# A third x buffer: all three state projections ahead of the tables and the latent tiles

## The chip, the cores and the metric

One core of a Trainium2 chip runs the kernel. The metric is device time in microseconds (us) of one execution, the median of several runs. The core has five engines with a queue each, which run their own instructions in order and wait for each other by semaphores: PE (matrix products), DVE (VectorE), ACT (ScalarE), POOL (GpSimd), and SP (SyncE), which here only issues DMA transfers. PEld is PE's loading of weights.

## What is computed

One step of a streaming encoder layer over 1152 positions (1024 of a new stream, 8 running streams with 16 each), all in float32:

```
xn  = RMSNorm(x)                         # x: 1152 x 1024
hin = xn @ w_in                          # -> q latent 384 | kv latent 256 | rope key 32 | S5 channels u 512
c_q, c_kv = RMSNorm(q_lat), RMSNorm(kv_lat)
o_a = attention(c_q, c_kv, rope key)     # 8 heads, chunk mask; running streams with their cache
bu  = B_bar u                            # S5: 32 groups of 16 channels, 64 complex states each
s   = associative_scan(lambda_bar, bu)   # over positions
o_b = GLU(gelu(Re(C s) + D u))
h   = x + concat(o_a, o_b) @ w_out
y   = h + ConvFFN(RMSNorm(h))
```

The change touches the first phase: the input projection `xn @ w_in`, the S5 tables (lambda_bar, B_bar and products of them) and the start of the S5 scan.

## The kernel before

A matmul operand is held as two halves, `hi` (rounded) and `lo` (the rest), and each product is three matmuls: hi hi, lo hi, hi lo (`mm3`, L138). `split` (L102, then L105 or L123) writes hi on ACT and lo on DVE or POOL.

Positions are cut into three blocks of 384 (block 2 holds the new stream's last 256 positions and the 128 of the running streams) and into nine latent tiles of 128 (block b has tiles 3b to 3b+2). `phase_a` works on transposed x:

- `load_x(b, k)` loads slice k of 8 of block b (`xs`, three buffers), splits it into `xhi`, `xlo` and sums squares into `accx`; `stats(b)` makes the norm factors `rx` and the row `Rb`.
- `load_w(k, hi, lo, c0)` loads slice k of the weights (`ws`, two buffers) and splits it. `wuh`, `wul` hold the 512 state columns, `wnh`, `wnl` the 672 latent columns. lo goes to DVE for even k and to POOL for odd k.
- `upart(b)` is the state projection of a block: 96 matmuls into four `up` banks, times `Rb` into `us` (two buffers) on DVE, stored to `u_dram`.
- `natpart(i)` is latent tile i: 48 matmuls into two `nat` banks, evicted by ACT, squares and square roots on ACT, two rsqrt chains of five small DVE steps each, two scalings on DVE, the rotation of `kpe` on POOL, stores to `cq_dram`, `ckv_dram` and the output. `nat` has two buffers.
- `tables()` makes the S5 tables: a long chain of small DVE steps, then products on POOL and DVE (`epre`, `tmpE`; `fo`, `tmpF`), PE transposes and products (`ep`, `kp`), stores to `e_dram`, `f_dram`, `kt_dram`.
- `s5_early` opens the tiles `Et` and `U` in the memory that the tables leave and loads `Et` from `e_dram`; `s5_load_u` loads `U` from `u_dram` in eight transfers (one for each position of a chunk of eight).
- `s5_states` makes the products `pst` of Et and U and evicts them into `RI` (`RI` on ACT and DVE, L423). Then `s5_scan` runs on DVE and POOL (steps `w`, `RI` at L105). `b8_open` and `b8_q` prepare the running streams' queries.

In the program the order is: load x 2 with wu, load x 0, load wn, `upart(2)`, `upart(0)`, tables, `s5_early`, latent tiles 8, 7, 6, load x 1 into the buffer that block 2 leaves, `upart(1)`, `s5_load_u`, `s5_states`, latent tiles 0 to 5 with b8 after tile 2. Blocks 2 and 1 share one buffer, block 0 has its own.

A scheduler that runs when the kernel is built moves instructions of one engine against each other, as their inputs come in its own model of time, and so the queues differ from the program text: the first steps of the tables, say, run among the x splits. Within a queue the order is then fixed. A tile that opens in memory that another has left waits for the last reader of that.

Of the kernel before, what the change touches and what calls it, by code (L numbers as in the profile page):

```python
# [75 lines left out]
def build(tc, t):  # L76
# [4 lines left out]
    with root:  # L81
# [43 lines left out]
        def split(hi, lo, src, scale=None, eng=None):  # L125
            if scale is None:
                acopy(hi, src)
                sub(lo, src, hi, eng)
            else:
                acopy(hi, src, scale)  # L130
                stt(lo, src, scale, hi.bitcast(F32), ALU.mult, ALU.subtract)
# [488 lines left out]
        def phase_a():  # L620
            st = ExitStack()
            with st:
                a = st.enter_context(tc.tile_pool(name="a", bufs=1))
                sg = st.enter_context(tc.tile_pool(name="asg", bufs=2))
                xb = None
                wnh = a.tile([P, 8, NATW], F32R, name="wnh")
                wnl = a.tile([P, 8, NATW], F32R, name="wnl")
                xhl, accx, al = {}, {}, {}

                def load_x(b, k):  # L630
                    if k == 0:
                        xp = xb if b == 0 else a
                        xhl[b] = (xp.tile([P, 8, TB], F32R, tag="xhi", name="xhi"),
                                  xp.tile([P, 8, TB], F32R, tag="xlo", name="xlo"))
                    s = al["p"].tile([P, TB], F32, tag="xs", name="xs", bufs=XB[0])
                    load(s, t["xT"][k * P:(k + 1) * P, b * TB:(b + 1) * TB])
                    split(xhl[b][0][:, k], xhl[b][1][:, k], s, gmix[:, k:k + 1])
                    if k == 0:
                        accx[b] = al["p"].tile([P, TB], F32, tag="accx", name="accx", bufs=1)
                        nc.scalar.activation(out=accx[b], in_=s, func=AF.Square)  # L640
                    else:
                        q = al["p"].tile([P, TB], F32, tag="sqx", name="sqx")
                        nc.scalar.activation(out=q, in_=s, func=AF.Square)
                        add(accx[b], accx[b], q, nc.gpsimd if b == 0 else None)

                def load_w(k, hi, lo, c0):
                    n = hi.shape[2]
                    w = al["p"].tile([P, NATW], F32, tag="ws", name="ws", bufs=XB[1])
                    load(w[:, 0:n], t["w_in"][k * P:(k + 1) * P, c0:c0 + n])
                    split(hi[:, k], lo[:, k], w[:, 0:n], eng=nc.gpsimd if k % 2 else None)  # L650

                gkv = a.tile([P, KL], F32, name="gkv")
                ss = a.tile([P, NT], F32, name="ss")
# [19 lines left out]
                def upart(b, kouter=False):  # L673
# [4 lines left out]
                    def step(cb_, k):  # L678
                        c0 = cb_ * P
                        if k == 0:  # L680
                            pu[cb_] = psum("u", [P, TB], "up")
                        mm3(pu[cb_], [((wuh[:, k, c0:c0 + P], wul[:, k, c0:c0 + P]), (xh[:, k], xl[:, k]))], first=k == 0, last=k == 7)

                    if kouter:
                        for k in range(8):
# [12 lines left out]
                def natpart(i):  # L698
# [6 lines left out]
                    jk = sg.tile([P, QL], BF16, tag="jk2", name="jk2", bufs=1)  # L705
                    for z, (c0, c1) in enumerate(((0, QL), (QL, NATW))):
                        p_ = psum("s", [P, c1 - c0], "nat")
                        mm3(p_, [((xh[:, k, tsl], xl[:, k, tsl]), (wnh[:, k, c0:c1], wnl[:, k, c0:c1])) for k in range(8)])
                        acopy(n[:, c0:c1], p_, rx[:, i:i + 1])
                        w = (QL, KL)[z]  # L710
                        nc.scalar.activation(out=jk[:, 0:w], in_=n[:, c0:c0 + w], func=AF.Square, accum_out=sq[:, z:z + 1])
                        rsqrt_act(sg, rq[:, z:z + 1], sq[:, z:z + 1], 1.0 / w, f"rq{z}")
                    cq, ck = n[:, 0:QL], n[:, QL:QL + KL]
                    ts(cq, cq, rq[:, 0:1], None, ALU.mult)
                    store(cq_dram[i * P:(i + 1) * P], cq)
# [10 lines left out]

                xbs = ExitStack()
                al["p"] = xbs.enter_context(tc.tile_pool(name="asl", bufs=2, reuse_waits="tile"))
                xb = xbs.enter_context(tc.tile_pool(name="xb", bufs=1, reuse_waits="tile"))
                ust = ExitStack()  # L730
                au = ust.enter_context(tc.tile_pool(name="au", bufs=1))
                wuh = au.tile([P, 8, SW], F32R, name="wuh")
                wul = au.tile([P, 8, SW], F32R, name="wul")
                for k in range(8):
                    load_x(2, k)
                    load_w(k, wuh, wul, NATW)
                load(ident, t["ident"])
                stats(2)
                for k in range(8):
                    load_x(0, k)  # L740
                late_consts()
                load(gkv, t["g_kv"])
                stats(0)
                for k in range(8):
                    load_w(k, wnh, wnl, 0)
                upart(2, True)
                upart(0, True)
                tables()
                s5_early()
                for i in (8, 7, 6):  # L750
                    natpart(i)
                for k in range(8):
                    load_x(1, k)
                stats(1)
                upart(1)
                ust.close()
                s5_open()
                s5_load_u()
                s5_states()
                for i in range(6):  # L760
                    natpart(i)
# [962 lines left out]
```

## Time and profile before

| | us |
|---|---|
| runs | 1563.75, 1566.25, 1566.29; median 1566.25 |
| the profiled execution | 1564.88 |
| its span, first to last instruction | 1563.1 |
| PE busy | 1470.5 (94%) |
| DVE busy | 1114.7 (71%) |
| ACT busy | 680.1 (44%) |
| POOL busy | 328.3 (21%) |
| mean granted clock of PE | 0.972 |

The span is cut into stages by time: up to some 58 us the x and weight splits with the first state projections, to 118 us the tables, to 175 us the third state projection and the first products of the S5 states, to 265 us the scan, and behind that attention, output projection and the ConvFFN, which is the larger part of the span. Busy times of an engine count instructions that run, also while such an instruction waits for a port; an idle engine that bounds nothing costs nothing. The granted clock is 1.00 at 2.4 GHz and 0.50 at 1.2 GHz.

### The profile page before, as it was taken

To read this page: it belongs to the slowest core of one execution; us is meant where nothing else is said; L and a number is where in the kernel's file an instruction comes from. 1 tells how busy PE (TensorE), PEld (TensorE's weight loads), DVE (VectorE), ACT (ScalarE), POOL (GpSimd) and SP (SyncE) were. 2 spreads that over 40 slices of the span, in tenths; PEclk is the share of its full clock that TensorE was granted. 3 is DMA by queue.
4 is the path that set the end of the run, shared out by engine and by line. 5 is a ranking of instruction groups with operands and counts; after the bars stand their busy time and mean duration, and the time that the engine had idled before them with its cause. 6 is when DMAs were issued, how large, how long until landed. Compare 5 with 4: busy or idle time off the path is not lost.

```text
span 1563.1 us, 23843 instructions
## 1 busy us (share of the span) xinstructions
PE 1470.5 (94%) x8733; PEld 1416.5 (91%) x8733; DVE 1114.7 (71%) x2372; ACT 680.1 (44%) x1323; POOL 328.3 (21%) x624
## 2 busy tenths in 40 slices
PE   6896866999989999999999999999999999999998
PEld 6876755877878999999999999999999999999998
DVE  8984799475778876468676666777767777667766
ACT  6342346666667886335333333333333333333321
POOL 3560466230355322112100000000000000000000
PEclk9998867999999999999999999999999999999999
DMA  7449434463221322630021111111111111111103
GB/s 201 123 150 153 126 122 87 100 199 103 79 91 49 95 72 77 212 101 28 25 71 41 42 41 41 42 51 44 43 50 44 41 41 41 42 41 41 41 1 132
DMA packets 101460, 122.15 MB, mean 78 GB/s; under 512 B 39524, under 2 KB 81636, under 8 KB 100868
## 3 DMA queue, kind: packets, MB, share of 16 engines
q1 hardware_dynamic: 100960, 120.44, 27.2%
q8 instruction: 68, 1.11, 0.3%
q14 instruction: 48, 0.39, 0.1%
q0 software_dynamic: 384, 0.20, 0.1%
HBM read 93.95 MB, written 26.65 MB: 77 GB/s over the span
## 4 chain that ended last, share of the span: by engine, by line
PE 76%; DVE 13%; DMA 5%; ACT 2%; issue 2%; SPq 2%; POOL 0%; DVEq 0%; ACTq 0%; POOLq 0%
PE pu L138 36%; PE pd L138 17%; PE pw L138 6%; DVE w L105 3%; PE pk L138 2%; PE pg L138 1%; PE pq L138 1%; PE po L1255 1%; SPq L96 1%; PE pst L1242 1%; PE pst L1243 1%; PE pst L1244 1%; PE po L1254 1%; PE po L1253 1%; DMA U<-u_dram 1%
## 5 line engine op out<-in xcount | busy, mean ns | idle before, releaser
L105 DVE TENSOR_TENSOR hT<-hT,pd 128x384 f32<-128x384 f32 x528 | 288.3, 551 | 218.4 <-PE pd L138 218.2
L138 PE MATMUL pu<-hnh,wh 128*128 128x384 f32 x1056 | 356.6, 338 | 0.0
L138 PE MATMUL pu<-hnl,wh 128*128 128x384 f32 x1056 | 356.4, 338 | 0.0
L138 PE MATMUL pu<-hnh,wl 128*128 128x384 f32 x1056 | 356.1, 337 | 0.0
L138 PE MATMUL pd<-act,wh 128*128 128x384 f32 x1056 | 348.7, 336 | 0.5 <-DVE hT L105 0.4
L1525 ACT ACTIVATE c<-pu,cvh 128x384 f32<-128x384 f32 x132 | 88.7, 672 | 309.0 <-PE pu L138 308.8
L138 PEld LDWEIGHTS pd<-act,wh 128*128 128x128 f32 x1056 | 197.7, 188 | 2.4 <-DVE hT L105 2.3
L138 PEld LDWEIGHTS pu<-hnh,wh 128*128 128x128 f32 x1056 | 198.4, 188 | 0.0
L138 PEld LDWEIGHTS pu<-hnl,wh 128*128 128x128 f32 x1056 | 198.3, 188 | 0.0
L138 PEld LDWEIGHTS pu<-hnh,wl 128*128 128x128 f32 x1056 | 198.0, 188 | 0.0
L123 DVE SCALAR_TENSOR_TENSOR c<-u,cvh,c 128x256 f32<-128x256 f32 (+1 forms) x352 | 171.2, 517 | 26.9 <-ACT u L102 13.7
L138 PE MATMUL pd<-act,wl 128*128 128x384 f32 x528 | 177.4, 336 | 0.0
L102 ACT ACTIVATE act<-c 128x384 fp32r<-128x384 f32 x66 | 34.7, 525 | 158.5 <-DVE c L105 158.5
L1531 POOL COPY u<-u 128x2 f32<-128x2 f32 x88 | 19.9, 227 | 384.6 <-DVE c L105 174.0
L138 PEld LDWEIGHTS pd<-act,wl 128*128 128x128 f32 x528 | 99.2, 188 | 0.0
L105 DVE TENSOR_TENSOR wl<-ws,wh 128x1024 fp32r<-128x1024 f32 x74 | 92.0, 1248 | 7.9 <-ACT wh L102 7.9
L102 ACT ACTIVATE wh<-ws 128x1024 fp32r<-128x1024 f32 x74 | 77.9, 1056 | 15.2 <-PE pw L138 8.8
L1543 POOL COPY cvo<-u 128x2 f32<-128x2 f32 x44 | 8.1, 184 | 355.2 <-ACT u L102 355.2
L1547 ACT ACTIVATE c<-c 128x384 f32<-128x384 f32 x66 | 34.6, 525 | 74.8 <-DVE c L123 74.7
L102 ACT ACTIVATE u<-pu 128x384 f32<-128x384 f32 (+2 forms) x176 | 66.3, 405 | 0.0
L138 PE MATMUL pw<-oh,wh 128*128 128x384 f32 x192 | 65.0, 340 | 0.2 <-DVE ql L123 0.2
L138 PE MATMUL pw<-oh,wl 128*128 128x384 f32 x192 | 64.4, 336 | 0.0
(461 smaller groups left out, 3122.9 us busy)
## 6 DMA issues: line engine op xcount, KB each, us to landing
ws<-in_w_up SPq DMA_DIRECT2D x44, 512.0 KB, 3.6
ws<-in_w_down SPq DMA_DIRECT2D x22, 512.0 KB, 3.5
xs<-in_xT SPq DMA_DIRECT2D x24, 192.0 KB, 3.5
os<-o_dram SPq DMA_DIRECT2D x24, 192.0 KB, 2.7
hT<-in_xT SPq DMA_DIRECT2D x24, 192.0 KB, 4.5
out_yT<-hT SPq DMA_DIRECT2D x24, 192.0 KB, 2.1
cf<-in_cT SPq DMA_DIRECT2D x8, 512.0 KB, 4.0
cn<-in_cn SPq DMA_DIRECT2D x8, 512.0 KB, 5.6
```

The costliest lines, as they stand in the source:

```text
L96: nc.sync.dma_start(out=out, in_=in_)
L102: nc.scalar.activation(out=out, in_=in_, func=AF.Copy, scale=scale)
L105: (eng or nc.vector).tensor_tensor(out=out, in0=a, in1=b, op=op)
L123: nc.vector.scalar_tensor_tensor(out=out, in0=a, scalar=s, in1=b, op0=op0, op1=op1)
L138: nc.tensor.matmul(out, lhsT=w, rhs=x, start=first and i == 0, stop=last and i == n - 1)
L1242: nc.tensor.matmul(o_, lhsT=kh[0:r, 4 * g + h, ks], rhs=qh[0:r, h, qs_], start=True, stop=False)
L1243: nc.tensor.matmul(o_, lhsT=kl[:, 4 * g + h, ks], rhs=qh[0:QD, h, qs_], start=False, stop=False)
L1244: nc.tensor.matmul(o_, lhsT=kh[0:QD, 4 * g + h, ks], rhs=ql[:, h, qs_], start=False, stop=True)
L1253: nc.tensor.matmul(po[:, qs_], lhsT=vhs, rhs=ph[:, sc_], start=f, stop=False)
L1525: nc.scalar.activation(out=c, in_=p_, func=AF.Identity, scale=w[2], bias=w[3])
L1531: nc.gpsimd.tensor_copy(out=u[:, 0:2], in_=halo[i, gv][:, TB:TB + 2])
L1547: nc.scalar.activation(out=g_, in_=g_, func=AF.Silu)
```

## The change

There is a third buffer for x, so that no block waits for another. The two halves of the weights are now lists of eight tiles each, one for a slice k and half; the state and the latent weights have the same tags (`wh0` and so on), so that slice k of the latent weights takes the memory of slice k of the state weights when its last projection has read that. In the program all x loads and all three state projections now come first, then the latent weights, the tables, `s5_early`, `s5_load_u`, and then the latent tiles 8, 7, 6; `s5_open`, `s5_states` and the tiles 0 to 5 follow as before. In `natpart` the two rsqrt chains are one chain over both columns; the square of a column is scaled before it is summed.

```diff
+                xpool = {1: a}
+                def wtiles(n, nm):
+                    return [[a.tile([P, n], F32R, tag=f"w{y}{k}", name=f"{nm}{y}{k}", padded_shape=[P, NATW]) for k in range(8)] for y in "hl"]
...
-                        xp = xb if b == 0 else a
+                        xp = xpool[b]
...
-                        nc.scalar.activation(out=jk[:, 0:w], in_=n[:, c0:c0 + w], func=AF.Square, accum_out=sq[:, z:z + 1])
-                        rsqrt_act(sg, rq[:, z:z + 1], sq[:, z:z + 1], 1.0 / w, f"rq{z}")
+                        nc.scalar.activation(out=jk[:, 0:w], in_=n[:, c0:c0 + w], func=AF.Square, scale=w ** -0.5, accum_out=sq[:, z:z + 1])
+                    rsqrt_act(sg, rq, sq, 1.0, "rq")
...
-                ust = ExitStack()
-                au = ust.enter_context(tc.tile_pool(name="au", bufs=1))
-                wuh = au.tile([P, 8, SW], F32R, name="wuh")
-                wul = au.tile([P, 8, SW], F32R, name="wul")
+                x2s = ExitStack()
+                xpool[2] = x2s.enter_context(tc.tile_pool(name="xc", bufs=1, reuse_waits="tile"))
+                wu = wtiles(SW, "wu")
                 for k in range(8):
                     load_x(2, k)
-                    load_w(k, wuh, wul, NATW)
+                    load_w(k, wu[0], wu[1], NATW)
                 load(ident, t["ident"])
                 stats(2)
                 for k in range(8):
                     load_x(0, k)
+                stats(0)
+                upart(2, True)
                 late_consts()
                 load(gkv, t["g_kv"])
-                stats(0)
-                for k in range(8):
-                    load_w(k, wnh, wnl, 0)
-                upart(2, True)
-                upart(0, True)
-                tables()
-                s5_early()
-                for i in (8, 7, 6):
-                    natpart(i)
                 for k in range(8):
                     load_x(1, k)
                 stats(1)
-                upart(1)
-                ust.close()
+                upart(0, True)
+                upart(1, True)
+                wn = wtiles(NATW, "wn")
+                for k in range(8):
+                    load_w(k, wn[0], wn[1], 0)
+                tables()
+                s5_early()
+                s5_load_u()
+                for i in (8, 7, 6):
+                    natpart(i)
+                x2s.close()
                 s5_open()
-                s5_load_u()
                 s5_states()
```

Three places show where the instructions stand. A number behind a name tells tiles of the same name apart.

SP's queue at the end of the tables, before (`Et`, `U`, `h0`: tiles of the scan; `nat_1503`: latent tile 0):

```order
L99 DMA kt_dram_64<-kts_948 16x512
L96 DMA Et_956<-e_dram_71 128x32x128
L96 DMA h0_1420<-in_h0 128x256
L99 DMA u_dram_63<-us_1395 1024x1x48
L99 DMA u_dram_63<-us_1398 1024x1x48
L99 DMA cq_dram_66<-nat_1503 128x384
L99 DMA u_dram_63<-us_1401 1024x1x48
L99 DMA u_dram_63<-us_1404 1024x1x48
L99 DMA ckv_dram_67<-nat_1503 128x256
L99 DMA out_ckv<-nat_1503 128x256
L96 DMA U_957<-u_dram_63 16x32x144 x8
```

The same place now (`nat_1188` is latent tile 8, `nat_1265` tile 7):

```order
L99 DMA out_ckv<-nat_1188 128x256
L99 DMA kt_dram_64<-kts_1124 16x512
L99 DMA kt_dram_64<-kts_1139 16x512
L99 DMA kt_dram_64<-kts_1154 16x512
L99 DMA kt_dram_64<-kts_1169 16x512
L96 DMA Et_1177<-e_dram_71 128x32x128
L96 DMA U_1178<-u_dram_63 16x32x144 x8
L99 DMA cq_dram_66<-nat_1265 128x384
```

The loads of U have moved up to Et, since the four stores of block 1's u are long past; the stores of tile 8 now stand ahead of the last four table stores.

PE's queue at the first products of the S5 states, before (`nat_1862` is latent tile 3; `x3` is a row of three like instructions):

```order
L138 MATMUL nat_1862<-wnh_94,xlo_1215 128x384
L138 MATMUL nat_1862<-wnl_95,xhi_1214 128x384
L421 MATMUL pst_1435<-U_957,Et_956 128x144 x3
L421 MATMUL pst_1441<-U_957,Et_956 128x144 x3
L421 MATMUL pst_1447<-U_957,Et_956 128x144 x3
```

And now (`nat_1538` is the end of latent tile 0, `nat_1588` is tile 1):

```order
L138 MATMUL nat_1538<-wnh7_748,xlo_239 128x288
L138 MATMUL nat_1538<-wnl7_756,xhi_238 128x288
L421 MATMUL pst_1439<-U_1178,Et_1177 128x144 x3
L421 MATMUL pst_1445<-U_1178,Et_1177 128x144 x3
L421 MATMUL pst_1451<-U_1178,Et_1177 128x144 x3
L421 MATMUL pst_1457<-U_1178,Et_1177 128x144 x3
L138 MATMUL nat_1588<-wnh0_741,xhi_238 128x384
```

Tiles 1 and 2, and the first nine matmuls of tile 3, stood ahead of the S5 products and now stand behind or among them.

POOL's queue at the start of the table products, before (`wnl` splits of the latent weights, `epre` and `tmpE` table products):

```order
L105 TENSOR_TENSOR wnl_95<-ws_316,wnh_94 128x672
L105 TENSOR_TENSOR accx_232<-accx_232,sqx_273 128x384
L105 TENSOR_TENSOR accx_232<-accx_232,sqx_280 128x384
L105 TENSOR_TENSOR wnl_95<-ws_324,wnh_94 128x672
L105 TENSOR_TENSOR wnl_95<-ws_332,wnh_94 128x672
L105 TENSOR_TENSOR wnl_95<-ws_340,wnh_94 128x672
L105 TENSOR_TENSOR epre_720<-LRr_702,bb1_693 128x4x128
```

And a stretch of the table products now:

```order
L105 TENSOR_TENSOR epre_980<-LRr_923,bb1_914 128x4x128
L105 TENSOR_TENSOR wnl1_750<-ws_761,wnh1_742 128x672
L105 TENSOR_TENSOR tmpE_981<-LIr_924,bb2_915 128x4x128
L105 TENSOR_TENSOR epre_993<-LRr_923,bb1_914 128x4x128
L105 TENSOR_TENSOR tmpE_994<-LIr_924,bb2_915 128x4x128
L105 TENSOR_TENSOR epre_1006<-LRr_923,bb1_914 128x4x128
L105 TENSOR_TENSOR tmpE_1007<-LIr_924,bb2_915 128x4x128
L105 TENSOR_TENSOR wnl3_752<-ws_769,wnh3_744 128x672
```

The four splits on POOL stood ahead of all table products and now stand among them.

## Rows read from the trace of the kernel before

**Rows 1.** The page's first part: busy us, share of the span, instructions.

```profile
PE 1470.5 (94%) x8733; PEld 1416.5 (91%) x8733; DVE 1114.7 (71%) x2372; ACT 680.1 (44%) x1323; POOL 328.3 (21%) x624
```

**Rows 2.** Stages: busy PE, PEld, DVE, ACT, POOL; granted clock; DMA share; GB/s.

```profile
58.00:100.00 42.00, 33.42 (x216) 29.85 (x214) 40.40 (x71) 17.13 (x42) 37.43 (x36) 1.00 0.45 135
...
118.00:135.00 17.00, 17.00 (x112) 16.95 (x111) 11.72 (x72) 5.52 (x15) 1.08 (x5) 1.00 0.81 202
135.00:158.00 23.00, 8.35 (x54) 8.05 (x53) 3.81 (x19) 3.47 (x13) 1.63 (x8) 0.73 1.15 131
...
175.00:265.00 90.00, 56.80 (x238) 45.56 (x237) 88.86 (x214) 37.97 (x89) 65.37 (x90) 0.77 0.35 94
265.00:430.00 165.00, 157.76 (x880) 136.94 (x880) 103.11 (x266) 109.43 (x200) 40.63 (x77) 0.96 0.41 114
```

**Rows 3.** The chain of waits, around 110 to 265 us: start, us, what.

```profile
132.17 2.74 DMA u_dram<-us
...
142.23 15.41 DMA U<-u_dram
...
159.77 8.05 DMA c<-ckv_dram
167.83 5.65 DMA gr<-in_g_kh
...
175.12 1.56 DVE w L105 x3
...
264.91 5.78 PE pk L138 x18
```

**Rows 4.** PE's waits, 100 to 180 us: total us, times, longest.

```profile
PE pst L421 <- DMA cq_dram<-nat: 14.7, 1, 14.7
```

**Rows 5.** SP's timeline: start, us, instruction.

```profile
117.28 0.60 SPq L96 DMA_DIRECT2D Et<-e_dram  x1
...
134.99 9.68 SPq L96 DMA_DIRECT2D U<-u_dram  x8
```

**Rows 6.** Stretches of 2 us, columns as in rows 2.

```profile
124.00:126.00 2.00, 2.00 (x18) 2.00 (x17) 2.00 (x11) 1.19 (x4) 0.00 (x0) 1.00 1.01 288
...
148.00:150.00 2.00, 0.00 (x0) 0.00 (x0) 0.00 (x0) 0.00 (x0) 0.00 (x0) 0.50 1.23 118
```

**Rows 7.** DVE's timeline, single instructions.

```profile
36.37 0.61 DVE L123 SCALAR_TENSOR_TENSOR xlo<-xs,gmix,xhi 128x384 fp32r<-128x384 f32 x1
...
38.22 0.85 DVE L105 TENSOR_TENSOR wnl<-ws,wnh 128x672 fp32r<-128x672 f32 x1
...
40.56 0.87 DVE L105 TENSOR_TENSOR us<-up,Rb 128x384 f32<-128x384 f32 x1
...
71.34 1.04 DVE L123 SCALAR_TENSOR_TENSOR rsw<-rq 128x1 f32<-128x1 f32 x1
...
133.79 0.15 DVE L120 TENSOR_SCALAR rsv<-sq 128x1 f32<-128x1 f32 x1
...
134.04 0.16 DVE L123 SCALAR_TENSOR_TENSOR rsw<-rq 128x1 f32<-128x1 f32 x1
...
134.62 0.42 DVE L118 TENSOR_SCALAR nat<-nat,rq 128x384 f32<-128x384 f32 x1
...
136.41 0.48 DVE L123 SCALAR_TENSOR_TENSOR nat<-nat,rq,gkv 128x256 f32<-128x256 f32 x1
...
163.01 1.23 DVE L105 TENSOR_TENSOR kn<-kn 128x1024 f32<-128x1024 f32 x1 [2.20 <-DMA kn<-in_krope]
```

**Rows 8.** POOL's timeline, one split of the latent weights.

```profile
43.40 1.64 POOL L105 TENSOR_TENSOR wnl<-ws,wnh 128x672 fp32r<-128x672 f32 x1 [5.56 <-ACT wnh L102]
```

**Rows 9.** Groups by line: busy us, mean ns, idle before, releaser.

```profile
L105 POOL TENSOR_TENSOR wnl<-ws,wnh 128x672 fp32r<-128x672 f32 x4 | 10.7, 2663 | 13.6 <-ACT wnh L102 13.6
```

**Rows 10.** PE's timeline at the S5 products.

```profile
157.83 5.43 PE L421 MATMUL pst<-U,Et 128*128 128x144 f32 x24 [14.65 <-DMA cq_dram<-nat]
...
167.23 1.63 PE L421 MATMUL pst<-U,Et 128*128 128x144 f32 x12
```

More of the change, by code (lines that the diff above doesn't have):

```diff
@@ L624, in phase_a @@
                 sg = st.enter_context(tc.tile_pool(name="asg", bufs=2))
-                xb = None
-                wnh = a.tile([P, 8, NATW], F32R, name="wnh")
-                wnl = a.tile([P, 8, NATW], F32R, name="wnl")
+                xpool = {1: a}
+                def wtiles(n, nm):
+                    return [[a.tile([P, n], F32R, tag=f"w{y}{k}", name=f"{nm}{y}{k}", padded_shape=[P, NATW]) for k in range(8)] for y in "hl"]
                 xhl, accx, al = {}, {}, {}
@@ L646, in load_w @@
                 def load_w(k, hi, lo, c0):
-                    n = hi.shape[2]
+                    n = hi[k].shape[1]
                     w = al["p"].tile([P, NATW], F32, tag="ws", name="ws", bufs=XB[1])
                     load(w[:, 0:n], t["w_in"][k * P:(k + 1) * P, c0:c0 + n])
-                    split(hi[:, k], lo[:, k], w[:, 0:n], eng=nc.gpsimd if k % 2 else None)
+                    split(hi[k], lo[k], w[:, 0:n], eng=nc.gpsimd if k % 2 else None)
                 gkv = a.tile([P, KL], F32, name="gkv")
@@ L681, in step @@
                             pu[cb_] = psum("u", [P, TB], "up")
-                        mm3(pu[cb_], [((wuh[:, k, c0:c0 + P], wul[:, k, c0:c0 + P]), (xh[:, k], xl[:, k]))], first=k == 0, last=k == 7)
+                        mm3(pu[cb_], [((wu[0][k][:, c0:c0 + P], wu[1][k][:, c0:c0 + P]), (xh[:, k], xl[:, k]))], first=k == 0, last=k == 7)
                     if kouter:
@@ L707, in natpart @@
                         p_ = psum("s", [P, c1 - c0], "nat")
-                        mm3(p_, [((xh[:, k, tsl], xl[:, k, tsl]), (wnh[:, k, c0:c1], wnl[:, k, c0:c1])) for k in range(8)])
+                        mm3(p_, [((xh[:, k, tsl], xl[:, k, tsl]), (wn[0][k][:, c0:c1], wn[1][k][:, c0:c1])) for k in range(8)])
                         acopy(n[:, c0:c1], p_, rx[:, i:i + 1])
                         w = (QL, KL)[z]
-                        nc.scalar.activation(out=jk[:, 0:w], in_=n[:, c0:c0 + w], func=AF.Square, accum_out=sq[:, z:z + 1])
-                        rsqrt_act(sg, rq[:, z:z + 1], sq[:, z:z + 1], 1.0 / w, f"rq{z}")
+                        nc.scalar.activation(out=jk[:, 0:w], in_=n[:, c0:c0 + w], func=AF.Square, scale=w ** -0.5, accum_out=sq[:, z:z + 1])
+                    rsqrt_act(sg, rq, sq, 1.0, "rq")
                     cq, ck = n[:, 0:QL], n[:, QL:QL + KL]
@@ L728, in phase_a @@
                 al["p"] = xbs.enter_context(tc.tile_pool(name="asl", bufs=2, reuse_waits="tile"))
-                xb = xbs.enter_context(tc.tile_pool(name="xb", bufs=1, reuse_waits="tile"))
-                ust = ExitStack()
-                au = ust.enter_context(tc.tile_pool(name="au", bufs=1))
-                wuh = au.tile([P, 8, SW], F32R, name="wuh")
-                wul = au.tile([P, 8, SW], F32R, name="wul")
+                xpool[0] = xbs.enter_context(tc.tile_pool(name="xb", bufs=1, reuse_waits="tile"))
+                x2s = ExitStack()
+                xpool[2] = x2s.enter_context(tc.tile_pool(name="xc", bufs=1, reuse_waits="tile"))
+                wu = wtiles(SW, "wu")
                 for k in range(8):
                     load_x(2, k)
-                    load_w(k, wuh, wul, NATW)
+                    load_w(k, wu[0], wu[1], NATW)
                 load(ident, t["ident"])
```

## The prediction

> **What bounds the kernel now.** I read the table by stage first [rows 1, 2]: PE is busy for 94% of the span, and from 265 us on for 157.76 of 165 us, so after that point a change in the first phase can only shift the rest. Before 265 us the stages have different limits. In 58 to 100 us, the S5 tables, DVE is busy 40.40 and POOL 37.43 of 42 us. In 135 to 158 us nothing computes: PE 8.35, DVE 3.81, ACT 3.47 of 23 us, while the DMA share is 1.15. In 175 to 265 us, the scan, DVE is busy 88.86 of 90 us and PE only 56.80. So two numbers decide: when the scan starts, and how much DVE work lies in it.
>
> The chain [rows 3] says what ends the hole: U<-u_dram, landing at 157.65. PE's one long wait in 100 to 180 us is 14.7 us in front of the first pst [rows 4]; the view names a cq_dram store, but that store was long done, the loads of U are what ended there. SP's queue [rows 5] shows why U is late: Et was issued at 117.28, when the last table was stored, U only at 134.99, because the third block of u was not in DRAM earlier. From its first issue U needs 157.65 - 134.99 = 22.7 us. While Et was under way the DMA moved 288 GB/s, during U 118 GB/s [rows 6].
>
> **What is moved off the path.** The state projection of block 1 (96 matmuls) goes ahead of the tables, with its eight x loads, splits and u stores. Three latent tiles stand between the tables and the first pst as before, plus tile 0; tiles 1 and 2, which stood ahead of pst, go behind its first matmuls. On SP the loads of U now follow Et directly. But they still follow it: Et waits for the last e_dram store and in the queue for the last kt_dram store, so U cannot be issued before the tables end. "State first" brings U to the table end, no further.
>
> **When the tables end.** I count DVE and POOL work up to that point, as those two are full [rows 2]. DVE gets four more us (0.87 each, 3.5 in all), the kn product (1.23) and a statistics step (some 1.5 by its like); it loses two latent tiles (each two chains from 133.79 to 134.62, 0.83, plus 0.42 and 0.48: 2.6) and one chain of tile 8: 3.5 + 1.2 + 1.5 - 5.2 - 0.8 = +0.2 us [rows 7]. POOL loses the rotations of two tiles (POOL's whole work in 118 to 135 us is 1.08 in five records, three of them one tile's [rows 2]): about -1.9. The weight splits are there in both. So by work the end stays at 117.3, and I take that. The order can move it. Early: the eight xlo of block 1 (0.61 each) lie among the last tables now and leave them, 4.9, and the two rotations go, 1.9: 110.5. Late: ahead of the tables DVE gets eight xlo and five additions of block 1 (at most as long as an xlo) and loses four wnl, 13 x 0.61 - 4 x 0.85 = +4.5 us, and the four POOL splits that now stand between the table products take 1.64 each where little disturbs them [rows 8], 6.6 in all: +11.1, 128.4.
>
> **When U lands.** Et is 2048 KB; at 288 GB/s that is 7.3 us of all DMA engines. U's loads are issued from 117.9 on and share the engines. I take the two one after the other, since the DMA share is about 1 or more under both [rows 6]: 117.9 + 7.3 + 22.7 = 147.9, 9.9 us before 157.83. The other end: U's small rows (118 GB/s) fit into gaps of Et, 117.9 + 22.7 = 140.6, 17.2 us earlier. PE is not later than that: behind the last table matmul stand about 100 latent matmuls, at 17.00 us for 112 records [rows 2] 15.2 us, so it is through at about 132. DVE and ACT idle there. Behind U's issues on SP stand the stores of tiles 7 and 6; tile 0 needs tile 7's buffer, and gets it within the hole. A hole of about 16 us thus stays, and it is PE's clock that suffers: after the hole the granted clock is 0.50 in 148 to 150 us [rows 6], the lower of the two levels, 1.2 GHz, and the first 24 pst records take 5.43 us, against 1.63 us for 12 later [rows 10].
>
> **From pst to scan.** Before: 157.83 to 175.12 [rows 3, 10], 17.3 us. In it the chain runs through loads of c8 (8.05 us) and gr (5.65), since two small DVE steps on the g vectors stand among the evictions. In the changed order these steps come seven scan steps later, and no transpose of b8 stands between the pst. What is left until the tenth group: 5.4 (24 records, slow) + 32 x 0.136 = 4.4 + 26 latent matmuls, at 15.2/100 each, 4.0, + one eviction 0.6 = 14.4, so 2.9 us saved. Lower end: all 26 at half speed, 4 us more, a loss of 1.1; upper end as taken, 2.9.
>
> **What the scan gets.** Tiles 1 to 5 instead of 3 to 5 lie there. Per tile 0.83 + 0.42 + 0.48 = 1.7 us of DVE now, 2.6 before (the joint rsqrt saves one chain, and nine square roots on ACT, which is not full): 5 x 1.7 - 3 x 2.6 = +0.7. POOL's rotations of two more tiles, 1.9 us, can hold DVE up for as long: +0.7 to +2.6, I take 2. PE gets 96 matmuls, 14.6 us, into 90 us with 33 us idle: hidden; if that cover fails it costs up to 14.6. The loads for b8 are now issued behind tile 2, later than before, but their first reader on DVE stands behind the seven scan steps, some 30 us on.
>
> **The sum.** 9.9 + 2.9 - 2.0 = 10.8 us. From the profiled execution, 1564.88, that is 1554.1; the median of the runs, 1566.25, is 1.4 above that execution, so I predict 1555.5. With the table end between 110.5 and 128.4 the gain is 17.6 to -0.3, with U fully beside Et 18.1.
>
> **A rule against the change.** In 58 to 100 us DVE and POOL are busy 77.8 us together in 42 [rows 2], and steps on 128x1 values take as long as a POOL step beside them (rsw 1.04 us at 71.34 against 0.16 at 134.04) [rows 7]: one engine's step waits for the other's. The Trainium skill, SBUF — State Buffer, section "SBUF: two separate sides", says that a DVE instruction with two SBUF inputs and a GpSimd instruction exclude each other for the whole instruction, the later one fully blocked. By it the four POOL splits, and with them the table end, cost their whole 1.64 each, and the sum would give 1562 instead of 1555.5; this trace agrees in kind, though the two busy times also count the waiting.
>
> **The rivals.** A, *the two loads overlap*: U lands at 140.6; 17.2 + 2.9 - 2 = 18.1, time 1548. For it: Et's share of the engines is not far above 1 and U's rows leave much of the bandwidth free. Against: the share under U is above 1 already.
>
> B, *the POOL splits lengthen the tables*: the four splits lie in the stretch where both engines are full, and each one's 1.64 us is added whole: table end +6.6, gain 4.2, time 1562.
>
> C, *the gain is given back*: the scan starts earlier, but the stretch up to 265 us waits for something that has not moved with it (b8's loads behind tile 2, PE's latent tiles in front of b8's products), so phase b starts as before: 1566. For it: PE's tiles before b8 grow by 14.6 us. Against: DVE, not PE, is full there.
>
> D, slower, *the shared tiles make a chain*: the split of wn tile k on ACT must wait until block 1's last projection has read wu tile k, and behind it in ACT's queue stand the factor Rb of block 1 and the evictions of the e tables; POOL's wn splits wait in front of its table products. Before, these four splits cost POOL 10.7 us plus 13.6 us of waiting [rows 9], all ahead of the tables. If both fall into the tables, they end 24.3 us later and the gain of 10.8 turns into a loss of 13.5: 1580. It decides from a table end of about 128 us on. Against it: the projection of block 1 should be through by some 75 us, when only the first table products are under way.
>
> That the change does not do what it says is ruled out by the orders, apart from U standing behind Et, which the sum holds.
>
> **How the numbers follow.** Forecast 0.50, A 0.15, B 0.13, C 0.12, D 0.10. A measurement of this kernel tells apart about 0.2%, 3.1 us: faster below 1563.1, slower above 1569.4. The forecast, A and somewhat over half of B are faster: 0.73; the rest of B, C and some of the forecast's late table ends are the same: 0.17; D is slower: 0.10. The range 1546 to 1567 holds the forecast with its table ends, A, B and C, and leaves out D.
>
> **What would show it.** Right: Et and U issued in one run at about 117 us (110 to 128), first pst at about 148, scan at about 162, the run of pk that the chain reaches at 264.91 [rows 3] at about 254, everything behind shifted by the same. PE's wait before the first pst stays, at about 15 us. Wrong: Et later than 128 (B, D; then POOL's wait for wnh in the table stretch is the row to read); pst at 141 (A); scan early but that pk not (C).

## The result, and the profile after

The changed kernel is slower: 1574.47 us, median of 5 runs (1572.30 to 1578.79), against 1566.29 (1563.75 to 1567.74) for the kernel before beside it, ratio 1.006 (95% interval 1.004 to 1.008). The forecast was 1555.5, in a range of 1546 to 1567. The profiled span went from 1563.1 to 1570.4 us.

Of the milestones that the forecast counted in, the first pst and the scan moved the way it said, but by about half. SP's timeline after (start, us, instruction) shows Et and U in one run, Et 3.8 us later and U 12.6 us earlier than in [rows 5]:

```profile
121.08 0.59 SPq L96 DMA_DIRECT2D Et<-e_dram  x1
122.37 19.72 SPq L96 DMA_DIRECT2D U<-u_dram  x8
142.19 2.20 SPq L99 DMA_DIRECT2D cq_dram<-nat  x1
...
183.83 0.32 SPq L96 DMA_DIRECT2D cq<-cq_dram  x1
...
237.60 0.44 SPq L99 DMA_DIRECT2D out_ckv<-nat  x1
238.14 0.58 SPq L96 DMA_DIRECT2D cf<-in_cT  x1
...
306.30 1.90 SPq L99 DMA_DIRECT2D y_dram<-U  x3
```

The chain of waits (start, us, what) then goes from U to the first pst at 153.44, against 157.83 [rows 10], and to the scan at 168.28, against 175.12 [rows 3]:

```profile
137.52 14.15 DMA U<-u_dram
151.69 1.75 DMA out_ckv<-nat
153.44 5.11 PE pst L421 x24
...
168.28 1.71 DVE w L105 x3
...
185.68 8.39 DMA wkT<-in_w_kT
...
261.87 6.13 DMA Tt<-kt_dram
```

The loss is in the lower half of SP's rows. The load `cq` for b8 and the first load of the next phase, `cf<-in_cT`, which were issued at 158.41 and 218.68 before, now go at 183.83 and 238.14. `cf` stands right behind the last store of the last latent tile (`out_ckv<-nat`, before 218.16). The first store of the S5 output, `y_dram`, comes at 306.30 instead of 300.17. So the S5 part starts 6.8 us earlier and gives its first output 6.1 us later.

The table by stage (busy PE, PEld, DVE, ACT, POOL; granted clock; DMA share; GB/s) shows why, read beside [rows 2]:

```profile
58.00:100.00 42.00, 34.41 (x181) 32.50 (x180) 37.67 (x55) 10.58 (x17) 31.42 (x22) 0.84 0.54 143
...
135.00:158.00 23.00, 4.58 (x21) 4.61 (x22) 1.22 (x2) 2.56 (x7) 0.86 (x4) 0.55 0.96 129
158.00:175.00 17.00, 17.00 (x118) 17.00 (x117) 12.52 (x26) 8.88 (x24) 3.73 (x6) 1.00 0.08 28
175.00:265.00 90.00, 62.46 (x297) 51.86 (x296) 86.96 (x216) 43.74 (x107) 66.07 (x106) 0.81 0.45 122
...
1100.00:1600.00 500.00, 465.38 (x2651) 464.07 (x2649) 327.51 (x612) 147.11 (x274) 34.87 (x142) 1.00 0.14 44
```

The same stretch before:

```profile
1100.00:1600.00 500.00, 458.05 (x2609) 456.76 (x2608) 321.12 (x602) 142.99 (x269) 34.60 (x141) 1.00 0.14 43
```

From 1100 us on PE has 465.38 us of work left, where it had 458.05 before: 7.33 us more, the 7.3 us by which the span grew. So the question is where PE lost time ahead of it.

A sum helps. For each 2 us I take the stretch less PE's busy time multiplied by the granted clock, so that both idle time and work at the lower level count as lost, and add up by stage:

| PE time lost, us | 0-58 | 58-118 | 118-158 | 158-175 | 175-265 | 265-340 | 340-410 | 0-410 |
|---|---|---|---|---|---|---|---|---|
| before | 15.3 | 11.2 | 14.7 | 2.4 | 46.8 | 8.7 | 5.1 | 104.2 |
| after | 17.2 | 17.0 | 20.9 | 0.0 | 39.1 | 8.2 | 6.1 | 108.6 |
| hole filled (e6) | 17.0 | 18.1 | 4.4 | 3.1 | 43.5 | 10.3 | 7.1 | 103.4 |
| latent lo on DVE (e8) | 17.4 | 11.3 | 17.2 | 0.0 | 39.8 | 8.1 | 3.8 | 97.6 |
| after again (e13) | 17.7 | 16.1 | 20.4 | 0.0 | 39.7 | 8.0 | 5.4 | 107.3 |
| last split on DVE (e14) | 16.6 | 14.1 | 20.7 | 0.0 | 40.9 | 8.4 | 1.9 | 102.7 |
| filled, U's rows long (e15) | 17.4 | 13.3 | 3.8 | 0.6 | 47.0 | 9.4 | 3.8 | 95.5 |

The change gains 10.1 us in 158 to 265 and loses 13.9 ahead of that: 5.8 in the table stretch, mostly by the clock (0.84 against 1.00 in 58 to 100 us), and 6.2 in the hole. Up to 410 us that is 4.4 of the 7.3; the rest lies behind, where this sum shows no single place. Taken for all seventeen traces, the span less this sum lies between 1458.9 and 1466.2 us, while the span itself goes from 1558.3 to 1586.0: what PE loses by 410 us mostly comes out at the end. Two traces of one kernel differ in the sum by 1.3 us (after and e13), 1.6 (e10 and e14) and 4.4 (e12 and e15), so a difference of 4 us between single traces is no proof by itself. Here two more traces stand on either side: e2, as fast as the kernel before, loses 99.7, and e4, as slow as the changed one, 111.1.

What PE lacks in the hole is latent tiles. These are the stretches again, for the matmuls into `nat` alone. Before:

```profile
118.00:135.00 17.00, 13.46 (x87) 1.00 0.81 202
135.00:152.00 17.00, 8.18 (x53) 0.81 1.14 118
```

After:

```profile
58.00:118.00 60.00, 19.94 (x92) 0.86 0.60 166
118.00:135.00 17.00, 15.61 (x100) 1.00 0.83 162
135.00:152.00 17.00, 0.00 (x0) 0.56 1.20 141
```

Of the 432 latent matmuls the trace before has 297 by 152 us, the one after 192. Block 1's projection, which stood in that hole, is now done among the tables, and nothing that could take its place is ready. There are two reasons. First, the latent weights come late. No tile can end before the last split on POOL, which ends at 104.27 in POOL's timeline; before, the last started at 56.63 and took 3.87 us. The latent matmuls, which began at 30.3 before, begin at 77.3:

```profile
74.73 2.09 POOL L105 TENSOR_TENSOR wnl<-ws,wnh 128x672 fp32r<-128x672 f32 x1
...
102.16 2.11 POOL L105 TENSOR_TENSOR wnl<-ws,wnh 128x672 fp32r<-128x672 f32 x1
104.24 7.24 POOL L105 TENSOR_TENSOR tmpF<-LI,m 128x576 f32<-128x576 f32 x3
111.44 0.25 POOL L105 TENSOR_TENSOR m<-nat,cosb 128x32 f32<-128x32 f32 x1
```

ACT's timeline shows where that begins. Its first hi half waits for PE's state projection, which still reads the shared tiles:

```profile
68.85 1.42 ACT L102 ACTIVATE wnh<-ws 128x672 fp32r<-128x672 f32 x2 [8.88 <-PE up L138]
```

Second, the queues behind U. In PE's queue tile 1 stands behind the first pst, so after tile 0 nothing is left to run. PE's waits, 100 to 180 us (total, times, longest), have 19.0 us in front of pst; [rows 4] had 14.7:

```profile
PE pst L421 <- DMA out_ckv<-nat: 19.0, 1, 19.0
```

The view names a store, as in [rows 4], but pst reads only Et and U: the last of U's eight loads is issued at 139.83 and takes 13.1 us to land, at 152.9. Had tile 1 stood ahead of pst, it would have been held up as well. The stores of a tile stand behind U's eight issues, which hold SP's queue from 122.37 to 142.09, and with two `nat` buffers tile 0 cannot be evicted before an older tile is stored. Experiment e1, whose PE has tiles 0 to 2 ahead of pst, shows that wait. In front of its evictions of `nat` (engine idle: us, times) ACT sat idle for

```profile
  DMA out_ckv<-nat: 24.3, 1
```

The 105 missing matmuls are then made in the scan, whose DVE also has the tiles' steps. The last latent matmul starts at 218.7 instead of 208.6, and behind it stand the last tile's stores and the loads of the next phase. ACT's first split of `cf` starts at 245.0 instead of 223.0, and PE's first `pk`, the product that reads it, at 247.2 instead of 229.2. PE's busy time with `pk` in the scan, before and then after:

```profile
175.00:265.00 90.00, 18.95 (x49) 0.77 0.35 94
175.00:265.00 90.00, 12.40 (x39) 0.81 0.45 122
```

So in the scan PE does 8.8 us more of latent tiles (29.27 against 20.44) and 6.6 us less of the next phase.

### The profile page after: what moved, and what is told of

Read it like the earlier page. It is cut to its first block, busy times and chain, and to the rows that moved or that the text cites. A ratio compares the mean times of both kernels' runs of the same rounds, so it can differ in the third digit from the quotient of the medians.

```text
span 1570.4 us, 23803 instructions
## 1 busy us (share of the span) xinstructions
PE 1473.5 (94%) x8733; PEld 1418.8 (90%) x8733; DVE 1109.4 (71%) x2327; ACT 678.1 (43%) x1315; POOL 327.2 (21%) x624
## 4 chain that ended last, share of the span: by engine, by line
PE 77%; DVE 11%; DMA 5%; ACT 3%; issue 1%; SPq 1%; POOL 1%; DVEq 0%; ACTq 0%; POOLq 0%
PE pu L138 35%; PE pd L138 17%; PE pw L138 6%; PE pk L138 2%; DVE w L105 2%; PE pg L138 1%; SPq L96 1%; PE pZ L1016 1%; PE pq L138 1%; PE po L1257 1%; PE pS L138 1%; PE pst L1244 1%; PE pst L1245 1%; PE pst L1246 1%; PE po L1255 1%
## 5 line engine op out<-in xcount | busy, mean ns | idle before, releaser
L102 ACT ACTIVATE wh<-ws 128x1024 fp32r<-128x1024 f32 x74 | 78.0, 1058 | 13.9 <-PE pw L138 8.0
```

The source lines that it names most:

```text
L102: nc.scalar.activation(out=out, in_=in_, func=AF.Copy, scale=scale)
```

## The experiments

My theory was that the late latent tiles, and not a late scan, are the loss. The rivals were that U behind Et is what counts (A turned round), the joint rsqrt chain, the POOL splits in the table stretch (B), the shared weight tiles (D), and a chance order elsewhere. "Tiles by 152" counts latent matmuls, "last" is the start of the last one, "phase b" the issue of `cf<-in_cT`. Each ratio is to the kernel before in the same set of runs; the sets are e1 to e4, e5 to e8, e9 to e12, e13 to e15.

| kernel | us | ratio (95%) | tiles by 152 | last | phase b | first pst | scan |
|---|---|---|---|---|---|---|---|
| before | 1566.25 | 1 | 297 | 208.6 | 218.7 | 157.8 | 175.1 |
| after | 1574.47 | 1.006 (1.004-1.008) | 192 | 218.7 | 238.1 | 153.4 | 168.3 |
| e1 | 1588.86 | 1.016 (1.014-1.019) | 192 | 202.7 | 207.9 | 185.6 | 212.8 |
| e2 | 1564.32 | 1.000 (0.9985-1.0015) | 311 | 203.5 | 215.1 | 157.8 | 175.3 |
| e3 | 1568.74 | 1.002 (1.001-1.003) | 192 | 218.5 | 237.7 | 151.5 | 168.4 |
| e4 | 1574.59 | 1.006 (1.004-1.008) | 192 | 218.0 | 237.4 | 152.3 | 167.5 |
| e5 | 1569.83 | 1.002 (1.0005-1.0036) | 220 | 214.5 | 226.4 | 151.5 | 166.5 |
| e6 | 1563.81 | 0.998 (0.9967-1.0001) | 288 | 205.4 | 215.7 | 151.9 | 170.8 |
| e7 | 1567.90 | 1.002 (1.000-1.004) | 288 | 206.0 | 215.7 | 151.5 | 171.4 |
| e8 | 1565.91 | 0.999 (0.998-1.001) | 240 | 208.5 | 220.3 | 151.4 | 167.0 |
| e9 | 1565.13 | 1.000 (0.998-1.001) | 288 | 202.5 | 212.8 | 152.4 | 167.6 |
| e10 | 1567.02 | 1.001 (0.9995-1.0024) | 192 | 217.1 | 237.0 | 151.0 | 166.3 |
| e11 | 1572.69 | 1.004 (1.002-1.006) | 192 | 213.9 | 233.3 | 149.3 | 163.6 |
| e12 | 1561.07 | 0.998 (0.996-0.9995) | 288 | 204.3 | 214.7 | 151.9 | 169.7 |
| e13 | 1573.34 | 1.004 (1.003-1.006) | 192 | 217.3 | 236.8 | 152.1 | 166.7 |
| e14 | 1566.76 | 1.001 (0.9996-1.0022) | 192 | 216.2 | 235.6 | 150.6 | 165.3 |
| e15 | 1560.88 | 0.997 (0.9955-0.998) | 288 | 201.1 | 211.4 | 151.1 | 166.3 |

**e1: tiles 0 to 2 and b8 written ahead of pst.**

```diff
+                for i in range(3):
+                    natpart(i)
+                xbs.close()
+                b8_open()
+                b8_q()
                 s5_states()
-                for i in range(6):
+                for i in range(3, 6):
```

> The kernel after, with latent tiles 0 to 2 and the loads and chain of b8 written ahead of the pst matmuls. In PE's order the first pst now stands behind tiles 0 to 3 instead of behind tile 0. Theory F (filler): the change used up the PE work that filled the wait for U (block 1's projection, tiles 1 and 2), and b8's loads, which stand behind tile 2's stores, and with them the first loads of phase b slid from 218.7 to 238.1 us. Then PE's idle time in 135 to 158 us falls from 18.4 to under 8, b8's loads are issued before 170 instead of 183.8, phase b's first cf load before 225, and the time is 1558 to 1566. Theory T (tables): the time is lost by the tables ending 3.8 us later and by block 1 standing among them; then the place of the tiles changes little: 1571 to 1576.

Neither theory's time came. The tiles end early (202.7) and phase b's loads are issued at 207.9, but the built order spread the pst groups over 185.6 to 209.6, the scan starts 44.5 us later than after, and the time is the worst of all. So an early end of the tiles is not enough; a late scan costs too, and the S5 chain does matter. The run doesn't isolate the tiles.

**e2, e3: the joint rsqrt put into the kernel before, and taken out of the changed one.**

```diff
-                        nc.scalar.activation(..., func=AF.Square, scale=w ** -0.5, accum_out=sq[:, z:z + 1])
-                    rsqrt_act(sg, rq, sq, 1.0, "rq")
+                        nc.scalar.activation(..., func=AF.Square, accum_out=sq[:, z:z + 1])
+                        rsqrt_act(sg, rq[:, z:z + 1], sq[:, z:z + 1], 1.0 / w, f"rq{z}")
```

That is e3; e2 is its reverse on the kernel before.

> The kernel before with only the joint rsqrt chain of the two latent columns. Theory F: 49 DVE and 9 ACT instructions less in a stretch where DVE is full, worth at most 2 us: 1564 to 1567. Rival J (the joint chain makes the first column wait for the second, so cq is stored later, and b8 and phase b with it): slower, 1568 to 1573.

> The kernel after with two rsqrt chains again. Theory F: 1573 to 1577, as after or up to 2 us slower. Rival J: most of the loss is undone, 1566 to 1570.

Alone it is worth nothing (1.000). Taken out of the changed kernel it gains 0.2 to 0.4% (1.002 against 1.006 and, in e13, 1.004), although every milestone up to 240 us stays. In the sum of lost time e3 loses 3.0 us in 340 to 410, after 6.1 and e13 5.4. That is the second cause, below; up to 410 us e3's sum, 107.3, is no smaller than that of e13, so it doesn't show the whole gain.

**e4: U issued ahead of Et.**

> The kernel after with U's eight loads issued ahead of Et's one. If both loads go one after the other, as the prediction took it, the first pst starts at 153 us within 1.5 as in the kernel after (it needs both), and the time is 1573 to 1576. If U's issues were held up by Et's transfer in front of them (they took up to 5.5 us each in the kernel after), both land earlier, pst starts at 146 to 150, and, if the hole sets the end, the time is 1566 to 1571; if it does not set the end, 1573 to 1576 all the same.

The edit moves `load(Et, e_dram)` behind `s5_load_u()`. SP's timeline shows U first, and how long the queue is held:

```profile
121.61 9.75 SPq L96 DMA_DIRECT2D U<-u_dram  x8
131.45 2.43 SPq L96 DMA_DIRECT2D Et<-e_dram  x1
133.98 14.19 SPq L99 DMA_DIRECT2D cq_dram<-nat  x1
```

First pst at 152.3, time unchanged. The two loads cost their sum in either order.

**e5, e6, e7: the hole filled.** e5 gives `nat` six buffers. e6 adds an order by hand on PE: tiles 8, 7, 6, 0, 1, 2, then pst. e7 is e6 with two rsqrt chains.

```diff
-                    n = sg.tile([P, NATW], F32, tag="nat", name="nat")
+                    n = sg.tile([P, NATW], F32, tag="nat", name="nat", bufs=6)
...
+                with tc.manual_schedule(engines={mybir.EngineType.PE}):
+                    for i in (8, 7, 6):
+                        natpart(i)
+                    x2s.close()
+                    s5_open()
+                    for i in range(3):
+                        natpart(i)
+                    xbs.close()
+                    b8_open()
+                    s5_states()
+                b8_q()
+                for i in range(3, 6):
+                    natpart(i)
```

> The kernel after with six buffers for a latent tile instead of two, which takes away what tile 0 waits for in the hole: in the kernel after and in e1 the eviction of the third and fourth tile waited until 152 us for out_ckv stores that stand behind U's issues on SP (122 to 142 us). Theory S (the stores behind U block the filler): PE runs tile 0 and part of tile 1 in 135 to 152 us, its idle time in 135 to 158 falls from 18.4 to 8 to 12 us; since the scan stretch idles on PE anyway, only part of that comes out at the end: 1568 to 1573. Rival (U alone sets everything up to the scan, and DVE everything behind it): PE's idle time falls and the time stays at 1573 to 1577.

> As e5, and PE's order written by hand so that tiles 0, 1 and 2 stand ahead of the first pst, with b8's loads behind them and b8's chain behind the pst matmuls, so that the scan is not pushed back as it was in e1 (first pst at 185.6 there). Theory S with F: PE idles under 6 us in 135 to 158, pst starts by 155, b8's loads are issued by 160 (183.8 in the kernel after), the first cf load of phase b by 222 (238.1), y_dram's first store by 300 (306.3), time 1561 to 1567. Rival (DVE is the bound from the scan on, so filler on PE brings nothing): the first cf load stays behind 232 and the time at 1572 to 1576.

> As e6, with two rsqrt chains per tile, which were worth 5.7 us in the kernel after (e3) and nothing in the kernel before (e2). If the joint chain costs because a tile holds its buffer and its stores longer while tiles wait for buffers, then with six buffers the two forms are equal within 2 us. If it costs by itself (the first column is normalized later, so cq is stored later), this is 4 to 6 us faster than e6: 1556 to 1562.

The same latent rows in 135 to 152 us, e5:

```profile
135.00:152.00 17.00, 2.17 (x14) 0.63 1.17 150
```

And e6:

```profile
135.00:152.00 17.00, 14.21 (x93) 1.00 1.18 154
```

With 93 matmuls in the hole the clock stays at 1.00 there, PE loses 4.4 us in 118 to 158 instead of 20.9, phase b's loads are issued at 215.7 instead of 238.1, and the time is 0.9984 of the kernel before, where the changed kernel had 1.006 and 1.0042. Buffers alone (e5) bring 14 matmuls and a part of it, 1.0021. First pst is at 151.9, no later: the hole was free room. Of the 16.5 us that e6 gains in 118 to 158, the other stretches up to 410 give 11.3 back, so the trace shows 5.2 of gain; it is of the longest of e6's ten executions, 1568.73, where the median is 1563.81. e7 is slower than e6 by 0.35% in their ratios, with intervals that just touch, and its trace loses as little (102.8). Neither of its expectations came; that two chains help in e3 and not here speaks for the order that a build gives, which isn't shown for e7.

**e8, e9: the latent lo halves on DVE,** alone and with e6.

```diff
-                    split(hi[k], lo[k], w[:, 0:n], eng=nc.gpsimd if k % 2 else None)
+                    split(hi[k], lo[k], w[:, 0:n], eng=nc.gpsimd if k % 2 and c0 else None)
```

> The kernel after with all eight lo halves of the latent weights made on DVE, none on POOL, so that no weight split stands between POOL's table products. Rival B of the prediction (the four POOL splits lengthen the tables by their whole time): the last kt_dram store, at 120.7 us in the kernel after, goes back to 115 to 118 and the time falls by 2 to 4 us. If DVE is the one that sets the table end, its four additional splits (0.85 us each) put the store at 122 to 125, and the time stays or rises by up to 3 us.

> e6 and e8 together: the hole filled by hand and all lo halves of the latent weights on DVE. Theory F (what counts is how many latent matmuls PE has done when U lands; by 152 us 194 in the kernel after, 303 in the kernel before, 246 in e8, 293 in e6): over 320 by 152 us, time 1555 to 1561, faster than both kernels. Rival (the two edits feed the same idle time of PE): as the better of the two, 1562 to 1566.

In e8 the tiles start no earlier (76.2 against 77.3) but get on faster; the latent rows of 58 to 118 us are

```profile
58.00:118.00 60.00, 27.13 (x130) 0.92 0.62 175
```

against 92 records after, and the last latent matmul is back at 208.5, phase b at 220.3, the time at 0.999. But Et is issued at 121.73, no earlier than after, so both halves of the expectation missed: the tables didn't end earlier, and the time fell all the same. What moving the splits brings is earlier tiles. What they add to the tables on POOL it doesn't tell, as DVE has four more splits in their place. Of the 11.0 us that e8's trace gains up to 410, 9.2 lie ahead of 158 us and 2.3 in the attention. e9 has both cures and no gain over either; its theory, over 320 matmuls by 152 us and 1555 to 1561, failed, and the rival's 1562 to 1566 came (the counts named there are 2 to 6 higher than this column, which is the trace's).

**e10, e14, e13: the last latent split alone, and the changed kernel again.** e10 and e14 are one kernel, which moves only slice 7's lo half to DVE (`k % 2 and (c0 or k < 7)`).

> The kernel after with only the last of the four POOL splits of the latent weights (slice 7) moved to DVE; in the kernel after it stood behind five tmpF products on POOL and ended at 104.2 us, and no latent tile can end before it. Theory F: most of e8's gain comes from this one split: first rotation of a latent tile on POOL at 97 to 101 us instead of 111.4, time 1565 to 1570. If e8's gain came from POOL's table products running without splits between them, about a quarter of it is seen: 1571 to 1574.

> e10 unchanged (only the last POOL split of the latent weights on DVE). In e10 the latent tiles and phase b were as late as in the kernel after (first cf load at 237.0 against 238.1), and yet the ratio was 1.0009 against 1.006. If that is a second cause (something behind 300 us), the ratio is again 0.999 to 1.003 and lies below e13 by at least 0.3%. If it was scatter between sets, e13 and e14 are within 0.2% of each other.

> The kernel after, unchanged, beside the kernel before and e14 on one chip. If the loss of 0.6% is the kernel's own, the ratio to the kernel before is again 1.004 to 1.008, as in its first measurement and in e4. If it was the set's, 1.000 to 1.003.

The tiles stay late (192, last 216 to 217, phase b 236 to 237) and still it gains, in one set: 1.0009 against 1.0042 for the changed kernel again. So the time came as expected for e10, but not for the reason given. Most of it is in the stretch 340 to 410 us, the attention. e13:

```profile
340.00:410.00 70.00, 64.64 (x362) 1.00 0.33 87
```

e14:

```profile
340.00:410.00 70.00, 69.02 (x386) 0.99 0.34 94
```

PE's longest wait there is for `PT`, after (and e13):

```profile
PE pZ L1016 <- ACT PT L102: 3.3, 2, 2.7
```

and e14:

```profile
PE pZ L1016 <- ACT PT L102: 1.0, 2, 0.7
```

PE's order differs: at the place of the long wait e14 has 18 `pg` products between the transposes of P and the `pZ` that needs them, and e13 has 12; at the next it is six and none. The edit touches no instruction of this part. The build's scheduler, given a slightly different first phase, wrote the attention in another order, and that is worth 3.5 us, some 0.2%, of the 4.6 that e14's trace gains on e13's by 410 us; 2.0 lie in the tables, where the edit is. Between before and after the attention counts for little: 5.1 and 6.1 us are lost in that stretch. And e14 does not clear the late tiles: ahead of 158 us it still loses 10.2 us more than the kernel before.

**e11, e12, e15: U stored with long rows;** e12 and e15 are one kernel, with e6 and e8 in it too.

```diff
-        u_dram = dram.tile([SW, LC, NCH], F32, name="u_dram")
+        u_dram = dram.tile([LC, GS, G, NCH], F32, name="u_dram")
...
-                load(s5t["U"][GS * j:GS * j + GS], u_dram.rearrange("(g c) j k -> j c g k", c=GS)[j])
+                load(s5t["U"][GS * j:GS * j + GS], u_dram[j])
...
-                        store(u_dram[cb_ * P:(cb_ + 1) * P, :, b * nck:(b + 1) * nck], us)
+                        store(u_dram[:, 4 * cb_:4 * cb_ + 4, :, b * nck:(b + 1) * nck].rearrange("j c g k -> (c g) j k"), us)
```

The state weights' columns are permuted to match while they are split.

> The kernel after with u kept in DRAM in the order slot, channel, group, position (the columns of the state weights are permuted when they are split), so that U's loads move rows of 18 KB instead of 576 bytes. The prediction's premise is that what the first phase gains at pst comes out at the end. U (2.36 MB) at the rate that Et showed, 288 GB/s, takes 8 us instead of 22.7: pst starts at 136 to 142 instead of 153.4, PE's hole falls from 18 to under 6 us. Premise: the time falls by 11 to 15, to 1559 to 1564. Theory F: PE's idle time falls as much, but b8's loads and tiles 3 to 5 still stand behind the scan's steps, so that part of it is given back: 1564 to 1569. If DVE alone is the bound from pst on, the whole 12 to 15 us come out.

> e9 and e11 together. With long rows U lands at about 138 us, where tiles 0 to 2, which stand ahead of pst by hand, are not through (152 us in e6), so pst waits for PE and not for U: pst at 146 to 152. Theory F: 1550 to 1558, the best of all. If filling the hole and shortening it are two ways to the same gain: 1557 to 1562, no better than e9.

> e12 unchanged, with more runs, since its interval (0.9958 to 0.9995) only just leaves out no change: 0.995 to 0.999 if the gain is real, 0.999 to 1.002 if not.

In e11 the first pst comes only 3 to 4 us earlier, not the 11 to 17 that were expected, though its rows are 18 KB, and the time, 1572.69, is above all that was expected. Two stretches, with Et under way and with U:

```profile
125.00:130.00 5.00, 5.00 (x32) 5.00 (x31) 3.02 (x21) 1.31 (x4) 0.87 (x4) 1.00 1.18 275
...
135.00:140.00 5.00, 0.00 (x0) 0.00 (x0) 0.00 (x0) 0.00 (x0) 0.00 (x0) 0.52 1.01 151
```

From the first issue to the last landing U takes 27.3 us, against 30.6 in the changed kernel. So row length is not the main part of what makes U slow. The kernel with all three edits beats both: 0.9976 and, again, 0.9968 (0.9955 to 0.998), the only one below 1 by an interval in two sets. Which of its edits adds how much over e6 isn't settled.

## Why the prediction was wrong, point by point

- **The bound: the failed reading.** "After that point a change in the first phase can only shift the rest" was right, and the time is PE's. But the two numbers I let decide, the start of the scan and DVE's work in it, leave out the third: how much of PE's own work is done by then. PE is busy 94% of the span, and over the traces most of what it loses early comes out at the end.
- **When the tables end.** Predicted 117.3 (110.5 to 128.4); Et is issued at 121.08, +3.8, inside the bounds.
- **U and Et.** Predicted one after the other, table end to pst 30.6 us; measured 153.44 - 121.08 = 32.4, with U landed after 31.8. e4, with the two turned round, has its first pst at 152.3. Rival A falls.
- **From pst to scan.** Predicted 14.4, measured 14.8. The scan is 6.8 us earlier, predicted 12.8: the tables and U took 3.8 and 1.8 us of it, pst 0.4.
- **The hole: right in sight, wrong in price.** I wrote that a hole of 16 us stays and that "it is PE's clock that suffers". It holds no latent matmul, 53 before, and the clock in 135 to 158 is 0.55. I priced that at nothing. (The row I gave for the clock "after the hole", 148 to 150 us, lies inside it.)
- **What the scan gets: the term that failed.** "PE gets 96 matmuls, 14.6 us, into 90 us with 33 us idle: hidden; if that cover fails it costs up to 14.6." It is 105 matmuls by the trace, as nine of tile 3 move too, and the cover failed. PE does use the idle time, 62.46 us busy against 56.80, but the tiles' DVE steps and stores run at the scan's pace, and in SP's queue the next phase's loads stand behind the last store: 19.5 us later. What PE gains in latent tiles there, 8.8 us, it mostly loses in `pk`, 6.6, which slides behind the scan. A cure of either reason (e6: 288 matmuls by 152 us; e8: 240) brings phase b's loads back to 216 and 220, and the time to that of the kernel before. I counted a resource that has room, not the queue behind it. I also priced b8's later loads at nothing, since their first reader on DVE is far off; PE reads them first, and waits 2.9 us for `cq` up to 186.14.
- **The gain that isn't there.** Instead of -10.8 us the change brought +8.2: 19.0 off. 6.0 of it is the scan, earlier by 6.8 and not 12.8. The tiles are 8 to 12 by ratios: e6 at 0.9984 and e8 at 0.9992, the changed kernel at 1.006 and 1.0042. e6's return lies in the hole and not in the attention (7.1 us lost there, more than after); e8's lies partly in the attention (3.8). The rest isn't settled.
- **The rule weighed, rival B.** The Trainium skill, SBUF — State Buffer, section "SBUF: two separate sides", lets a DVE instruction with two SBUF inputs and a GpSimd instruction exclude each other. This trace agrees in kind. DVE's timeline after has one split beside POOL's of 74.73, 2.30 us long, against 0.85 where nothing disturbs it [rows 7]:

```profile
75.24 2.30 DVE L105 TENSOR_TENSOR wnl<-ws,wnh 128x672 fp32r<-128x672 f32 x1
```

  Its forecast, tables 6.6 us later and 1562, isn't what came: they end 3.8 later, and the loss lies elsewhere. What the splits add to the tables stays open, since e8 puts them on DVE and the tables end as late.
- **Rival C** named the mechanism, "PE's tiles before b8", and b8's loads behind tile 2 (158.41 to 183.83). I gave it 0.12 and ended it at zero. Its sign came: the scan is early and pk is not. It goes past zero, as the latest tiles carry the next phase's loads. In PE's queue the first `pk` also stands behind b8's `pq`, which waits for DVE's `qal` up to 243.46 (224.42 before), so b8's late loads and phase b's end within 4 us of each other there, and no run separates them. My reason against, "DVE, not PE, is full there", is as I read it why the tiles were slow in the scan.
- **Rival D** had the sign and the first link of its chain: ACT's first latent split waits 8.88 us for block 1's projection. The rest didn't come: the tables end before 128, and POOL doesn't wait for `wnh` there. What the late weights hold up are the latent tiles. No run gives the latent weights memory of their own, so the share of the shared tiles isn't known.

Open: why e9 gains nothing over e6 and e8; how much of the tiles' lateness is the shared weight tiles; and where the 3 us behind 410 are lost.

## What to carry to other kernels

Where one engine is busy nearly all the time, price every step that is moved by what that engine has done by each milestone, and count the matmuls left for a hole ahead of a critical load: such a hole is room, not loss, as long as ready work stands in front of it. Cover is more than idle time in a stretch: follow the last item of the moved work down its own queue, and see which loads of the next phase stand behind its stores. Where a build's scheduler orders the program, a small edit can rewrite places far away, here for some 0.2%; a gain of that size is the edit's own only if the trace shows it where the edit is.

## What the runs showed of the hardware

- Long rows did not make a load fast: U moved at about 151 GB/s with rows of 18 KB (e11), 118 with short ones [rows 6], Et at 275 to 288. Each of U's loads writes 16 partitions, Et 128. Whether that is the cause wasn't tried.
- An issue held its queue longer behind a large load that was still under way: U's eight issues took 19.72 us on SP behind Et, 9.68 before [rows 5], and in e4 a single store behind Et took 14.19.
- The granted clock fell in the table stretch too, 0.84 on the mean of 58 to 100 us with PE busy 34.41 of 42, where it had been 1.00 with 33.42. By stretches of 2 us it is at 0.61 and 0.54 in 58 to 62, after PE was busy 3.46 of the 6 us before, and at 0.50, the lower level, in 94 to 98, after 6.63 of the 14 from 80 on.
